# Weight sums of the seven-product blocks moved from GpSimd to VectorE, one norm over all tokens, and its values copied out of PSUM

## The chip, the cores and the metric

One core of a Trainium2 chip (trn2). The metric is the device time of one execution in microseconds (us), the median of several runs. The core's engines are named as in the profile: PE (TensorE, matmuls), DVE (VectorE), ACT (ScalarE), POOL (GpSimd) and SP (SyncE, which issues nearly all DMAs here). Each engine works through its own list of instructions in order, and waits on semaphores of the others.

## The reference, cut to what matters

One layer of a decoder for 576 tokens (512 of a prompt, 64 of samples), in float32: a half-step SwiGLU FFN, a token mixing with three branches, and another half-step FFN. The change touches the two FFNs and the norms at their two ends.

```python
D_MODEL = 1024; D_FF = 2816
def _rmsnorm(x, g):
    return x * lax.rsqrt(jnp.mean(x * x, axis=-1, keepdims=True) + RMS_EPS) * g
def _swiglu(x, w_up, w_down):
    hg = x @ w_up
    return (jax.nn.silu(hg[..., :D_FF]) * hg[..., D_FF:]) @ w_down
x = x + 0.5 * _swiglu(_rmsnorm(x, ffn1_norm), ffn1_w_up, ffn1_w_down)
m = _token_mixing(_rmsnorm(x, mix_norm), ...);  x = x + m
x = x + 0.5 * _swiglu(_rmsnorm(x, ffn2_norm), ffn2_w_up, ffn2_w_down)
y = _rmsnorm(x, final_norm)
```

## The kernel before, in words

Activations lie with channels on the 128 partitions and tokens on the free axis: a tile is 128 x 576, and is worked on in two halves of H = 288 tokens, since a PSUM bank takes 512 values. A float32 operand is split into two parts of the type fp32r (`split`, L95): ACT casts the high part (L96), and VectorE subtracts it from the value for the low part (L97). A product is then three matmuls: high by high, high by low, low by high (`mm3k`, L108, its matmuls at L110).

**An FFN** (`ffn`, L394) goes over 22 blocks of 128 hidden channels. Each block takes two tiles of up-weights (one for the silu side, one for the other), gives a hidden tile, and hidden tiles go into the down projection by groups of 6, 4, 4, 4 and 4 blocks (L447 adds the result to x). A group's down tiles are computed behind the next group's blocks, two for each block of a group of four.

- The first five blocks (`plain`, L434) multiply x·g that isn't yet normed, so that PE can start before the norm is known. The norm's factor rn of each token is applied when results leave PSUM: VectorE takes q·rn into t1 (L438), ACT applies silu (L439), GpSimd multiplies t1 by rn once more (L440), since the other side lacks that factor too, and VectorE multiplies the other side out of PSUM by t1 (L442).
- The other 17 blocks (`strassen`, L351) use seven half-size products over normed operands (`operands`, L320) in place of eight. Four sums of weight tiles are needed for a block, made by `total` (L357) on GpSimd: a21+a22 and a11+a21 read loaded weight tiles alone ("p<-w" in the profile; a11 and a12 lie in the block's first tile, a21 and a22 in its second), the two others read a sum and a weight tile ("p<-p,w"). `product` (L362) splits a sum or a weight tile into a pair (wh, wl) and runs 12 matmuls (L369). Results leave PSUM by ACT's copy m1 (L379) and VectorE's L380, L382, L384, L388 and L391; the first product of bank pb must be read (L380) before the t3 product may add to that bank. L471 multiplies the block's two sides.
- **The norm** (`norm`, L405): squares are summed over the channels' tiles on ACT and VectorE; PE sums them over partitions, 128 tokens at a time (L138, 128 x 1 each); VectorE, ACT and VectorE turn them into 1/sqrt (L299, L300 with a load of ACT's function table, L301); PE spreads the values over the partitions (L148), and ACT copies them to SBUF (L309). Before, this goes by halves: three pieces for each (128, 128 and 32 tokens), six in all.
- **The end of an FFN** (L481 on): the last group's down projections run half by half. The first half's norm is taken in between, and the next step's norm starts on it (`done`: `mix_norm`, L557, after the first FFN; `final`, L1106, after the second). There the factors stay in PSUM and are read from there (L563 in `mix_norm`).

Four pools of buffers matter: 4 buffers for loaded weight tiles (w), 4 for split pairs, 4 for sums (p), and 8 PSUM banks. The framework's scheduler sets each engine's order when the kernel is built, by its own cost model; so a move of work to another engine also moves its neighbours' order.

Of the kernel before, what the change touches and what calls it, by code (L numbers as in the profile page):

```python
# [6 lines left out]
F32 = mybir.dt.float32  # L7
F32R = mybir.dt.float32r
AF = mybir.ActivationFunctionType
ALU = mybir.AluOpType  # L10
# [8 lines left out]
N = SEQ + NB * TS  # L19
H = N // 2  # L20
# [30 lines left out]
class _Builder:  # L51
# [240 lines left out]
    def xg(self):  # L292
        return [[self.xp.tile([128, N], F32R, name=f"x{2 * k + i}") for i in range(2)] for k in range(8)]

    def rstd(self, fp, ss, h):

        q = self.sums("p", [ss], self.con("ones", 1), slice(h * H, (h + 1) * H))
        t = fp.tile([128, 3], F32, name="rt", bufs=2)
        self.V.tensor_scalar(t, q, 1.0 / D, 1e-6, ALU.mult, ALU.add)  # L299
        self.A.activation(t, t, AF.Sqrt)  # L300
        self.V.reciprocal(t, t)  # L301
        return t

    def rows(self, fp, t, h, r=None):

        (_, p), = self.spread("p", t.unsqueeze(2).broadcast_to([128, 3, 128]), slice(h * H, (h + 1) * H))
        if r is None:
            return p
        self.A.copy(r, p)  # L309
        return r  # L310

    def sumsq(self, fp, ss, x, k, s):
# [38 lines left out]
    def strassen(self, fp, w, xs):  # L351


        V, G, A = self.V, self.G, self.A
        a11, a12, a21, a22 = (t.rearrange("p (k e c) -> p k e c", e=2, c=128)[:, :, e, :] for t in w for e in range(2))

        def total(u, v):  # L357
            s = self.sp.tile([128, N], F32, name="p")[:, :512].rearrange("p (k c) -> p k c", c=128)
            G.tensor_tensor(s, u, v, ALU.add)  # L359
            return s  # L360

        def product(p, src, b, first):  # L362
            hl = self.wparts()
            v = [t.rearrange("p (k c) -> p k c", c=128) for t in hl]
            self.split(v[0], v[1], src)
            for k in range(4):
                c = slice(128 * k, 128 * k + 128)
                for q, (l, o) in enumerate(((0, 0), (0, 1), (1, 0))):
                    self.T.matmul(p, hl[l][:, c], xs[k][b][:, o], start=first and k == 0 and q == 0,  # L369
                                  stop=k == 3 and q == 2, skip_group_check=True)  # L370

        pa, pb, pc = (self.bank()[:, :H] for _ in range(3))
        m1 = fp.tile([128, H], F32, name="m1")
        t1, t2 = (fp.tile([128, N], F32, name=n) for n in ("t1", "t2"))
        p1 = total(a21, a22)
        p2 = total(p1, a11)
        product(pb, p2, "t2", True)
        product(pa, a11, "b11", True)
        A.copy(m1, pa)  # L379
        V.tensor_tensor(t1[:, H:], pb, m1, ALU.subtract)  # L380
        product(pc, p1, "t1", True)
        V.tensor_tensor(t2[:, H:], pc, m1, ALU.add)  # L382
        product(pb, total(a11, a21), "t3", False)
        V.tensor_tensor(t2[:, H:], pb, t2[:, H:], ALU.subtract)  # L384
        product(pa, a12, "b21", False)
        A.activation(t1[:, :H], pa, AF.Silu)
        product(pc, total(p2, a12), "b22", False)
        V.tensor_tensor(t1[:, H:], pc, t1[:, H:], ALU.subtract)  # L388
        A.activation(t1[:, H:], t1[:, H:], AF.Silu)
        product(pb, a22, "t4", False)  # L390
        V.tensor_tensor(t2[:, :H], pb, m1, ALU.subtract)  # L391
        return t1, t2

    def ffn(self, x, hp, fp, g, wu, wd, done, raw=None, mid=None, kv=()):  # L394
# [4 lines left out]
        V, A = self.V, self.A  # L399
        room = lambda s: [(self.xp if s < 8 else hp).tile([128, N], F32R, name=f"x{2 * s + i}") for i in range(2)]  # L400
        xg = self.xg()
        ss = self.sp.tile([128, N], F32, name="p")
        rn = fp.tile([128, N], F32, name="rn", bufs=1)

        def norm():  # L405
            for k in range(0 if not raw else 4, 8):
                self.sumsq(fp, ss, x[k], k, slice(0, N))
            r = [self.rstd(fp, ss, h) for h in range(2)]
            return [self.rows(fp, t, h, rn[:, h * H:(h + 1) * H]) for h, t in enumerate(r)]

        for k in range(8):
            gk = self.par(g, k)
# [2 lines left out]
            if raw:  # L415
# [7 lines left out]
                if k == 7:  # L423
                    r = norm()
# [3 lines left out]
        if not raw:  # L428
            pre = [self.proj(wu[i], xg) for i in range(2)]
            r = norm()  # L430
            pre.append(self.proj(wu[2], xg))
        up = lambda i: pre[i] if i < 3 else self.proj(wu[i], xg)

        def plain(f):  # L434

            t1, t2 = (fp.tile([128, N], F32, name=n) for n in ("t1", "t2"))
            for (c, q), ri in zip(up(2 * f), r):
                V.tensor_tensor(t1[:, c], q, ri, ALU.mult)  # L438
            A.activation(t1, t1, AF.Silu)  # L439
            self.G.tensor_tensor(t1, t1, rn, ALU.mult)  # L440
            for c, q in up(2 * f + 1):
                V.tensor_tensor(t2[:, c], q, t1[:, c], ALU.mult)  # L442
            return hidden(f, t2)

        def down(m, h, f0):
            for c, p in self.proj(wd[m, :, f0 * 128:(f0 + len(h)) * 128], h, len(h)):
                V.scalar_tensor_tensor(x[m][:, c], p, 0.5, x[m][:, c], ALU.mult, ALU.add)  # L447

        def hidden(f, t2):
            hj = room(ROOMS[f])  # L450
            self.split(hj[0], hj[1], t2)
            return hj

        first, xs = [], []
# [6 lines left out]
        for n in FGROUPS:  # L461
            h = []
            for j in range(n):
                f = f0 + j
                if f < PLAIN:
                    h.append(first[f])
                else:
                    w = nxt
                    nxt = self.raws(wu, f + 1) if f + 1 < NF else None
                    t1, t2 = self.strassen(fp, w, xs)  # L470
                    V.tensor_tensor(t2, t2, t1, ALU.mult)  # L471
                    h.append(hidden(f, t2))
                for m in behind[8 * j // n:8 * (j + 1) // n]:
                    m()
            behind = [(lambda m=m, h=h, f0=f0: down(m, h, f0)) for m in range(8)]
            f0 += n
        if mid:
            mid()
        w = []
        for m in range(8):  # L480
            o = self.xe.tile([128, 2, 2, H], F32R, name=("t1", "b11")[m // 4] + str(m % 4))  # L481
            w.append([o[:, i].rearrange("p i c -> p (i c)")[:, :n * 128] for i in range(2)])
            q = self.wtile()[:, :n * 128]
            self.dma(q, wd[m, :, (NF - n) * 128:])
            self.split(w[m][0], w[m][1], q)
        ss = self.sp.tile([128, N], F32, name="p")
        for i in range(2):
            s = slice(i * H, (i + 1) * H)
            for m in range(8):
                p = self.bank()[:, :H]  # L490
                self.mm3(p, lambda q, f, t: w[m][q][:, f:t], h, n, i)
                V.scalar_tensor_tensor(x[m][:, s], p, 0.5, x[m][:, s], ALU.mult, ALU.add)
                self.sumsq(fp, ss, x[m], m, s)
                if i == 1 and m == 2:
                    r = self.rstd(fp, ss, 0)
                if i == 1 and m == 4:
                    done(x, fp, slice(0, H), self.rows(fp, r, 0))
        if kv:
            kv[0]()
        r = self.rstd(fp, ss, 1)  # L500
        if kv:
            kv[1](0)
        r = self.rows(fp, r, 1)
        if kv:
            kv[1](1)
        done(x, fp, s, r)
# [725 lines left out]
```

## Time and profile before

| | |
|---|---|
| runs | 1503.19, 1508.43 and 1508.97 us, median 1508.43 |
| the profiled execution | 1504.17 us; its span from first to last instruction 1502.4 us |
| mean granted PE clock | 0.982 |
| PE busy | 97% of the span |
| VectorE busy | 67% |
| ACT busy | 45% |
| GpSimd busy | 14% |

The two FFNs take the first and the last part of the span (GpSimd, which works in them only, is busy up to slice 10 of 40 and again from slice 29), token mixing the middle. In a row of the profile, "x2" after a form is a run of equal instructions, the two numbers at its start are the time since the span's start and the duration in us, and brackets at its end give the idle time of the engine just before, and which engine's instruction ended it. A window's row gives the window, its width, the busy time of PE, PE's weight loads, VectorE, ACT and GpSimd, then the granted PE clock, the DMA engines' busy share and GB/s. A group's row gives the count, the busy time, the mean duration in ns, and the idle time before.

### The profile page before, as it was taken

What the parts mean: (1) busy time and instruction counts of PE and PEld (TensorE: products, weight loads), DVE (VectorE), ACT (ScalarE), POOL (GpSimd) and SP (SyncE); (2) the same over time, 40 slices, a digit from 0 to 9 for tenths busy, and PEclk for the clock granted to TensorE, in tenths of its full rate; (3) what the DMA queues carried; (4) which work ended last, traced back from release to release, by engine and by line L of the source; (5) the groups of instructions that cost most, each with busy time, mean ns of one, the idle gap of its engine ahead of it and who ended that gap; (6) DMA issues with size and microseconds to landing.
All of it is one profiled execution on the core that took longest, in us unless ns stands there. A gap on an engine that the chain in (4) does not pass through costs nothing.

```text
span 1502.4 us, 27187 instructions
## 1 busy us (share of the span) xinstructions
PE 1464.7 (97%) x10786; PEld 1380.1 (92%) x10786; DVE 1012.8 (67%) x1911; ACT 672.6 (45%) x1369; POOL 212.7 (14%) x167
## 2 busy tenths in 40 slices
PE   8989999999989999999999999999999999999997
PEld 8989999999988799888888878789999999999997
DVE  7976666666783569769456456356578766767665
ACT  6434333434566645445346542443344333444342
POOL 1233233222000000000000000000014222222310
PEclk9999999999999999999899999999999999999998
DMA  6223222223632154123223134255222322223231
GB/s 207 71 71 99 85 85 85 85 85 100 205 92 96 41 154 90 46 79 107 60 58 108 54 96 127 91 185 176 85 71 71 91 79 85 89 92 103 85 85 63
DMA packets 95034, 144.05 MB, mean 96 GB/s; under 512 B 43628, under 2 KB 53228, under 8 KB 94908
## 3 DMA queue, kind: packets, MB, share of 16 engines
q1 hardware_dynamic: 94332, 141.74, 30.6%
q8 instruction: 84, 1.38, 0.4%
q10 hardware_dynamic: 576, 0.59, 0.1%
q14 instruction: 42, 0.34, 0.1%
HBM read 126.07 MB, written 16.23 MB: 95 GB/s over the span
## 4 chain that ended last, share of the span: by engine, by line
PE 89%; DVE 5%; ACT 2%; issue 1%; DMA 1%; SPq 0%; DVEq 0%; ACTq 0%
PE p L110 51%; PE p L369 24%; DVE wl L97 2%; PE g L874 1%; PE c L1008 1%; ACT wh L96 1%; PE c L1012 1%; PE c L1005 1%; DVE pr L967 1%; PE g L128 1%; PE c L128 1%; PE c L1040 1%; PE p L148 1%; PE c L1038 1%; DMA w<-win 1%
## 5 line engine op out<-in xcount | busy, mean ns | idle before, releaser
L110 PE MATMUL p<-x,wh 128*128 128x288 f32 x3136 | 656.7, 301 | 5.1 <-ACT x L96 4.7
L110 PEld LDWEIGHTS p<-x,wh 128*128 128x128 f32 x3136 | 508.3, 189 | 19.0 <-issue 7.5
L110 PE MATMUL p<-x,wl 128*128 128x288 f32 x1568 | 470.3, 300 | 1.4 <-DVE wl L97 1.4
L97 DVE TENSOR_TENSOR wl<-w,wh 128x512 fp32r<-128x512 f32 (+1 forms) x353 | 270.9, 770 | 139.0 <-ACT wh L96 131.8
L96 ACT CAST wh<-w 128x512 fp32r<-128x512 f32 (+1 forms) x353 | 209.2, 599 | 245.1 <-PE p L369 109.4
L110 PEld LDWEIGHTS p<-x,wl 128*128 128x128 f32 x1568 | 296.0, 189 | 6.9 <-issue 3.1
L369 PE MATMUL p<-t,wh 128*128 128x288 f32 x1088 | 224.4, 299 | 7.6 <-DVE t L380 7.3
L369 PEld LDWEIGHTS p<-t,wh 128*128 128x128 f32 x1088 | 173.8, 188 | 15.5 <-DVE t L380 15.5
L369 PE MATMUL p<-b,wh 128*128 128x288 f32 x816 | 170.3, 295 | 0.6 <-ACT m L379 0.6
L369 PE MATMUL p<-t,wl 128*128 128x288 f32 x544 | 160.5, 295 | 0.0
L97 DVE TENSOR_TENSOR wl<-p,wh 128x512 fp32r<-128x512 f32 x136 | 109.6, 806 | 71.1 <-ACT wh L96 69.4
L359 POOL TENSOR_TENSOR p<-w 128x512 f32<-128x512 f32 x68 | 95.1, 1399 | 361.1 <-DVE wl L97 170.3
L96 ACT CAST wh<-p 128x512 fp32r<-128x512 f32 x136 | 84.2, 620 | 127.5 <-PE p L110 71.2
L369 PEld LDWEIGHTS p<-b,wh 128*128 128x128 f32 x816 | 132.8, 188 | 1.0 <-ACT m L379 0.9
L369 PE MATMUL p<-b,wl 128*128 128x288 f32 x408 | 120.4, 295 | 0.0
L440 POOL TENSOR_TENSOR t<-t,rn 128x576 f32<-128x576 f32 x10 | 17.8, 1789 | 715.8 <-ACT t L439 715.8
L359 POOL TENSOR_TENSOR p<-p,w 128x512 f32<-128x512 f32 x68 | 96.5, 1419 | 59.2 <-DVE wl L97 46.0
L369 PEld LDWEIGHTS p<-t,wl 128*128 128x128 f32 x544 | 102.4, 188 | 0.0
L369 PEld LDWEIGHTS p<-b,wl 128*128 128x128 f32 x408 | 76.8, 188 | 0.0
L96 ACT CAST x<-t 128x576 fp32r<-128x576 f32 (+1 forms) x60 | 36.4, 609 | 83.0 <-DVE t L471 69.1
L447 DVE SCALAR_TENSOR_TENSOR x<-p,x 128x288 f32<-128x288 f32 x128 | 56.6, 449 | 12.4 <-PE p L110 12.4
L97 DVE TENSOR_TENSOR x<-t,x 128x576 fp32r<-128x576 f32 (+1 forms) x60 | 44.3, 743 | 14.0 <-ACT x L96 13.6
(346 smaller groups left out, 2008.7 us busy)
## 6 DMA issues: line engine op xcount, KB each, us to landing
w<-wu SPq DMA_DIRECT2D x85, 512.0 KB
w<-win SPq DMA_DIRECT2D x44, 512.0 KB
w<-wd SPq DMA_DIRECT2D x64, 256.0 KB
w<-wd SPq DMA_DIRECT2D x16, 384.0 KB
d_mb<-gate SPq DMA_DIRECT2D x16, 288.0 KB
w<-wo SPq DMA_DIRECT2D x8, 512.0 KB
x<-x SPq DMA_DIRECT2D x8, 288.0 KB
d_x<-x SPq DMA_DIRECT2D x16, 144.0 KB
```

What stands on the lines that cost most here:

```text
L96: self.A.copy(hi, x)
L97: self.V.tensor_tensor(lo, x, hi.bitcast(F32), ALU.subtract)
L110: self.T.matmul(p, l, x[r][:, c], start=k == 0 and i == 0, stop=k == n - 1 and i == 2)
L128: self.T.matmul(p, l, r[:, c], start=i == 0, stop=i == len(ops) - 1)
L148: self.T.matmul(p[:, o + f - d.start:o + 128 - d.start], r[f:, i], self.con("ident")[f:, f:], start=True, stop=True)
L359: G.tensor_tensor(s, u, v, ALU.add)
L369: self.T.matmul(p, hl[l][:, c], xs[k][b][:, o], start=first and k == 0 and q == 0, stop=k == 3 and q == 2, skip_group_check=True)
L440: self.G.tensor_tensor(t1, t1, rn, ALU.mult)
L447: V.scalar_tensor_tensor(x[m][:, c], p, 0.5, x[m][:, c], ALU.mult, ALU.add)
L874: T.matmul(ps[:, i * 128:(i + 1) * 128], kb[o, c + i].rearrange("p a t -> p (a t)"), ra[o, c + i].rearrange("p a t -> p (a t)"), start=Tru ...
L967: V.tensor_tensor(pr, tt[:, :n, :e].unsqueeze(2).broadcast_to([np_, n, m, e]), l3[:, t:e, :e].unsqueeze(1).broadcast_to([np_, n, m, e]), A ...
L1005: T.matmul(ps[64:, 64 * h:64 * h + 64], gr[:64, h, c, 64:], vu[:64, c, 64 * h:64 * h + 64], start=h == 0 or not inter, stop=not inter)
```

## The change

Four things are changed.

1. `total` runs on VectorE: 136 sums of 128 x 512 (four for each of 34 blocks).
2. In `plain`, both sides leave PSUM times rn, and `hidden` multiplies them on VectorE (as L471 did for the other blocks). GpSimd's L440 is gone, and with it GpSimd's last work in the FFNs.
3. `norm` takes all 576 tokens at once: five pieces in place of six, one pass of VectorE, ACT and VectorE over them, and two copies (512 and 64 tokens).
4. At an FFN's end the first half's factors are copied by ACT to rn in SBUF, and in the first FFN the second half's too; there `mix_norm` reads SBUF. In the second FFN the last half's factors stay in PSUM as before.

```diff
-    def rstd(self, fp, ss, h):
-        q = self.sums("p", [ss], self.con("ones", 1), slice(h * H, (h + 1) * H))
-        t = fp.tile([128, 3], F32, name="rt", bufs=2)
+    def rstd(self, fp, ss, c):
+        q = self.sums("p", [ss], self.con("ones", 1), c)
+        t = fp.tile([128, 5], F32, name="rt", bufs=2)[:, :q.shape[1]]
...
-    def rows(self, fp, t, h, r=None):
-        (_, p), = self.spread("p", t.unsqueeze(2).broadcast_to([128, 3, 128]), slice(h * H, (h + 1) * H))
-        if r is None:
-            return p
-        self.A.copy(r, p)
+    def rows(self, t, c, r=None):
+        for d, p in self.spread("p", t.unsqueeze(2).broadcast_to([128, t.shape[1], 128]), c):
+            if r is None:
+                return p
+            self.A.copy(r[:, d.start - c.start:d.stop - c.start], p)
         return r
...
-            G.tensor_tensor(s, u, v, ALU.add)
+            V.tensor_tensor(s, u, v, ALU.add)
...
-            r = [self.rstd(fp, ss, h) for h in range(2)]
-            return [self.rows(fp, t, h, rn[:, h * H:(h + 1) * H]) for h, t in enumerate(r)]
+            c = slice(0, N)
+            self.rows(self.rstd(fp, ss, c), c, rn)
+            return [rn[:, h * H:(h + 1) * H] for h in range(2)]
...
-            for (c, q), ri in zip(up(2 * f), r):
-                V.tensor_tensor(t1[:, c], q, ri, ALU.mult)
-            A.activation(t1, t1, AF.Silu)
-            self.G.tensor_tensor(t1, t1, rn, ALU.mult)
-            for c, q in up(2 * f + 1):
-                V.tensor_tensor(t2[:, c], q, t1[:, c], ALU.mult)
-            return hidden(f, t2)
+            for i, t in enumerate((t1, t2)):
+                for (c, q), ri in zip(up(2 * f + i), r):
+                    V.tensor_tensor(t[:, c], q, ri, ALU.mult)
+                if i == 0:
+                    A.activation(t1, t1, AF.Silu)
+            return hidden(f, t1, t2)
...
-        def hidden(f, t2):
+        def hidden(f, t1, t2):
             hj = room(ROOMS[f])
+            V.tensor_tensor(t2, t2, t1, ALU.mult)
             self.split(hj[0], hj[1], t2)
...
-                    r = self.rstd(fp, ss, 0)
+                    r = self.rstd(fp, ss, slice(0, H))
                 if i == 1 and m == 4:
-                    done(x, fp, slice(0, H), self.rows(fp, r, 0))
+                    done(x, fp, slice(0, H), self.rows(r, slice(0, H), rn[:, :H]))
...
-        r = self.rows(fp, r, 1)
+        r = self.rows(r, s, rn[:, H:] if kv else None)
```

In the changed file L439 is the step out of PSUM times rn (for both sides), L450 the product in `hidden`, and L446 what L447 was; L359 and L380 to L391 keep their numbers.

The order on VectorE in the first FFN, from the last step of the plain blocks to the first seven-product block's L382, before. Names ending in a number are buffers: wl a low half of a pair, w a loaded weight tile, p a sum or a PSUM bank, x24 and x25 a hidden tile's two parts.

```order
L442 TENSOR_TENSOR t2_831<-p_906,t1_830 128x288
L97 TENSOR_TENSOR wl_1035<-p_996,wh_1034 128x512
L442 TENSOR_TENSOR t2_831<-p_931,t1_830 128x288
L97 TENSOR_TENSOR wl_1054<-p_1051,wh_1053 128x512
L97 TENSOR_TENSOR x25_959<-t2_831,x24_958 128x576
L97 TENSOR_TENSOR wl_1071<-w_982,wh_1070 128x512
L97 TENSOR_TENSOR wl_1090<-p_1087,wh_1089 128x512
L380 TENSOR_TENSOR t1_994<-p_991,m1_993 128x288
L382 TENSOR_TENSOR t2_995<-p_992,m1_993 128x288
```

The same place on VectorE after:

```order
L439 TENSOR_TENSOR t2_824<-p_923,rn_183 128x288
L97 TENSOR_TENSOR wl_1047<-p_1044,wh_1046 128x512
L450 TENSOR_TENSOR t2_824<-t2_824,t1_823 128x576
L359 TENSOR_TENSOR p_1187<-w_979,w_980 128x512
L97 TENSOR_TENSOR wl_1064<-w_975,wh_1063 128x512
L97 TENSOR_TENSOR x25_951<-t2_824,x24_950 128x576
L97 TENSOR_TENSOR wl_1083<-p_1080,wh_1082 128x512
L380 TENSOR_TENSOR t1_987<-p_984,m1_986 128x288
L359 TENSOR_TENSOR p_1223<-p_1134,w_979 128x512
L382 TENSOR_TENSOR t2_988<-p_985,m1_986 128x288
```

The step out of PSUM no longer stands behind GpSimd's product, but the product in `hidden` and a sum for the next block (reading w_979 and w_980) now stand ahead of L380, and another sum behind it.

A seven-product block in the middle of the first FFN on VectorE, from its L384 on, before:

```order
L384 TENSOR_TENSOR t2_2110<-p_2106,t2_2110 128x288
L97 TENSOR_TENSOR wl_2247<-w_2244,wh_2246 128x512
L97 TENSOR_TENSOR wl_2281<-w_2278,wh_2280 128x512
L388 TENSOR_TENSOR t1_2109<-p_2107,t1_2109 128x288
L97 TENSOR_TENSOR wl_2327<-p_2324,wh_2326 128x512
L391 TENSOR_TENSOR t2_2110<-p_2106,m1_2108 128x288
L97 TENSOR_TENSOR wl_2343<-w_2101,wh_2342 128x512
```

The same block on VectorE after:

```order
L384 TENSOR_TENSOR t2_2103<-p_2099,t2_2103 128x288
L97 TENSOR_TENSOR wl_2240<-w_2237,wh_2239 128x512
L97 TENSOR_TENSOR wl_2274<-w_2271,wh_2273 128x512
L359 TENSOR_TENSOR p_2315<-w_2095 128x512
L388 TENSOR_TENSOR t1_2102<-p_2100,t1_2102 128x288
L359 TENSOR_TENSOR p_2317<-p_2315,w_2094 128x512
L359 TENSOR_TENSOR p_2370<-w_2094,w_2095 128x512
L391 TENSOR_TENSOR t2_2103<-p_2099,m1_2101 128x288
L97 TENSOR_TENSOR wl_2320<-p_2317,wh_2319 128x512
```

Three sums for the next block now stand between this block's last steps out of PSUM. The first of them reads a weight tile that a DMA has just brought, and stands ahead of L388.

The norm of the second FFN on PE, between the second and third up-projection, before:

```order
L110 MATMUL p<-x_12129,wh 128x288
L110 MATMUL p<-x_12128,wl 128x288
L138 MATMUL p<-cst,p 128x1 x6
L148 MATMUL p<-cst,rt 128x128 x2
L148 MATMUL p<-cst,rt 128x32
L148 MATMUL p<-cst,rt 128x128 x2
L148 MATMUL p<-cst,rt 128x32
L110 MATMUL p<-x_12114,wh 128x288
```

The same place on PE after:

```order
L110 MATMUL p<-x_12124,wh 128x288
L110 MATMUL p<-x_12123,wl 128x288
L138 MATMUL p<-cst,p 128x1 x5
L148 MATMUL p<-cst,rt 128x128 x4
L148 MATMUL p<-cst,rt 128x64
L110 MATMUL p<-x_12109,wh 128x288
```

Six sums and six spreads have become five and five; their place is the same, and nothing else stands between the sums and the spreads.

More of the change, by code (lines that the diff above doesn't have):

```diff
@@ L351, in strassen @@
     def strassen(self, fp, w, xs):
-        V, G, A = self.V, self.G, self.A
+        V, A = self.V, self.A
         a11, a12, a21, a22 = (t.rearrange("p (k e c) -> p k e c", e=2, c=128)[:, :, e, :] for t in w for e in range(2))
@@ L469, in ffn @@
                     nxt = self.raws(wu, f + 1) if f + 1 < NF else None
-                    t1, t2 = self.strassen(fp, w, xs)
-                    V.tensor_tensor(t2, t2, t1, ALU.mult)
-                    h.append(hidden(f, t2))
+                    h.append(hidden(f, *self.strassen(fp, w, xs)))
                 for m in behind[8 * j // n:8 * (j + 1) // n]:
@@ L494, in ffn @@
                 if i == 1 and m == 2:
-                    r = self.rstd(fp, ss, 0)
+                    r = self.rstd(fp, ss, slice(0, H))
                 if i == 1 and m == 4:
-                    done(x, fp, slice(0, H), self.rows(fp, r, 0))
+                    done(x, fp, slice(0, H), self.rows(r, slice(0, H), rn[:, :H]))
         if kv:
             kv[0]()
-        r = self.rstd(fp, ss, 1)
+        r = self.rstd(fp, ss, s)
         if kv:
             kv[1](0)
-        r = self.rows(fp, r, 1)
+        r = self.rows(r, s, rn[:, H:] if kv else None)
         if kv:
```

## The prediction

> **What bounds the kernel now.** I read the page first, then the waits of PE for the whole run, then the same by stretch, then PE's, VectorE's and GpSimd's timelines where PE waits.
>
> ```profile
> PE 1464.7 (97%) x10786; PEld 1380.1 (92%) x10786; DVE 1012.8 (67%) x1911; ACT 672.6 (45%) x1369; POOL 212.7 (14%) x167
> 100.00:420.00 320.00, 319.80 (x2385) 316.19 (x2384) 219.09 (x384) 134.06 (x255) 79.18 (x56) 1.00 0.33 101
> 1110.00:1480.00 370.00, 366.46 (x2728) 362.46 (x2727) 265.01 (x424) 149.60 (x273) 98.76 (x71) 1.00 0.27 83
> ```
>
> PE is the bound. In 320 us of the first FFN (second row) it is busy for all but 0.2 us at clock 1.00; in 370 us of the second it misses 3.5 us. In such stretches a faster VectorE or an idle GpSimd is worth nothing. The change drops six norm matmuls and no others; the rest of a gain must be PE's idle time or clock.
>
> ```profile
> PE p L369 <- DVE t L380: 7.3, 8, 2.5
> PE p L369 <- ACT m L379: 0.6, 1, 0.6
> PE p L369 <- DVE t L380: 3.9, 2, 2.5
> PE p L369 <- DVE t L380: 3.4, 6, 1.4
> 80.42 0.40 PE L369 MATMUL p<-b,wh 128*128 128x288 f32 x1 [0.64 <-ACT m L379]
> 83.29 0.54 PE L369 MATMUL p<-t,wh 128*128 128x288 f32 x2 [2.48 <-DVE t L380]
> 96.25 0.53 PE L369 MATMUL p<-t,wh 128*128 128x288 f32 x2 [1.42 <-DVE t L380]
> ```
>
> The first two rows are PE's waits inside seven-product blocks over the whole run: total us, times, longest. The third is the part from 60 to 105 us, the fourth that from 1085 us on. So they lie in the first blocks of each FFN: 0.64 + 2.48 + 1.42 = 4.5 us in the first, 3.4 in the second, 7.9 together. PE waits for L380 to empty a PSUM bank. Why L380 is late, VectorE and GpSimd show:
>
> ```profile
> 76.90 0.46 DVE L442 TENSOR_TENSOR t<-p,t 128x288 f32<-128x288 f32 x1 [1.31 <-POOL t L440]
> 77.27 0.68 DVE L97 TENSOR_TENSOR wl<-p,wh 128x512 fp32r<-128x512 f32 x1
> 77.87 0.45 DVE L442 TENSOR_TENSOR t<-p,t 128x288 f32<-128x288 f32 x1
> 78.24 1.69 DVE L97 TENSOR_TENSOR wl<-p,wh 128x512 fp32r<-128x512 f32 x1
> 79.85 0.75 DVE L97 TENSOR_TENSOR x<-t,x 128x576 fp32r<-128x576 f32 x1
> 80.52 1.75 DVE L97 TENSOR_TENSOR wl<-w,wh 128x512 fp32r<-128x512 f32 x1
> 82.19 0.68 DVE L97 TENSOR_TENSOR wl<-p,wh 128x512 fp32r<-128x512 f32 x1
> 82.79 0.45 DVE L380 TENSOR_TENSOR t<-p,m 128x288 f32<-128x288 f32 x1
> 74.99 1.87 POOL L440 TENSOR_TENSOR t<-t,rn 128x576 f32<-128x576 f32 x1
> 78.09 1.29 POOL L359 TENSOR_TENSOR p<-p,w 128x512 f32<-128x512 f32 x1 [1.22 <-issue]
> 80.01 1.72 POOL L359 TENSOR_TENSOR p<-w 128x512 f32<-128x512 f32 x1 [0.63 <-DVE wl L97]
> ```
>
> The reader is to see two things. VectorE stood idle for 1.31 us until GpSimd's L440 was done. And the same subtraction of 128 x 512 takes 0.68 us alone but 1.69 and 1.75 us when a GpSimd sum lies beside it (78.09 to 79.38; 80.01 to 81.73): 1.01 + 1.07 = 2.08 us lost. L442, which reads PSUM, isn't stretched.
>
> **The change part by part.** VectorE's load first, since 136 sums move there.
>
> ```profile
> L97 DVE TENSOR_TENSOR wl<-w,wh 128x512 fp32r<-128x512 f32 x320 | 255.7, 801 | 127.1 <-ACT wh L96 120.3 <-ACT xs L1010 0.9 <-ACT rt L300 0.3
> L97 DVE TENSOR_TENSOR wl<-p,wh 128x512 fp32r<-128x512 f32 x136 | 109.6, 806 | 71.1 <-ACT wh L96 69.4
> 92.11 0.75 DVE L471 TENSOR_TENSOR t<-t,t 128x576 f32<-128x576 f32 x1
> ```
>
> A sum on VectorE is not in the trace; its nearest row is L97 of the same 128 x 512 with two SBUF operands, 0.68 alone, so 136 x 0.68 = 92.5 us, and 10 products of the plain blocks at 0.75 (L471 alone), 7.5. Back come the stretches: 320 x (0.801 - 0.68) + 136 x (0.806 - 0.68) = 55.9 us. VectorE goes from 1012.8 to 1012.8 + 92.5 + 7.5 - 55.9 = 1057 us, or some us less where the 576-wide steps are freed of stretch too, GpSimd to near nothing in the FFNs. No moved step issues a DMA, so no queue of SP or GpSimd changes its list. The densest stretch is 1110 to 1480: 17 blocks x 4 x 0.68 = 46 on 265 makes 311 of 370 even with no stretch given back. Where PE is full, all this is hidden under it.
>
> **The stalls.** In the first FFN's first block the new order puts, after the last step out of PSUM, a subtraction, L450, a sum, and three more subtractions (one of 128 x 576) ahead of L380: 0.68 + 0.75 + 0.68 + 0.68 + 0.74 + 0.68 = 4.2 us of durations, about 3.7 by the rows' start-to-start spacing (77.27 to 77.87 for a 0.68). Without L440's wait the last step out of PSUM can end some 1.3 us earlier than in L442's chain, near 75.4, so L380 starts at 79.1 to 79.6 and ends by 80.0, not 83.2. PE wanted that bank 2.48 us before 83.29, at 80.81, and m1's matmul 0.64 before 80.42, at 79.78: the latter needs a pair that ACT and VectorE can have ready at about 79.4. I keep 0.3 us a FFN, 0.6 of the 7.9: -7.3. Bounds: 0 (VectorE stays late all the same) and -7.9.
>
> In later blocks three sums stand between L384 and L391. What hides them: after the seventh product (12 matmuls at 319.80 / 2385 = 0.134, 1.6 us) stand two down tiles of the previous group, and PE's 100 to 420 row has no wait to start from. The first sum waits for a weight DMA at the head of VectorE's queue, with L388 behind it:
>
> ```profile
> 220.22 1.29 POOL L359 TENSOR_TENSOR p<-w 128x512 f32<-128x512 f32 x1 [11.83 <-DMA w<-wu]
> 220.65 0.46 DVE L388 TENSOR_TENSOR t<-p,t 128x288 f32<-128x288 f32 x1 [0.39 <-PE p L369]
> L359 POOL TENSOR_TENSOR p<-p,w 128x512 f32<-128x512 f32 x68 | 96.5, 1419 | 59.2 <-DVE wl L97 46.0 <-issue 5.9 <-DMA w<-wu 2.3
> L359 POOL TENSOR_TENSOR p<-w 128x512 f32<-128x512 f32 x68 | 95.1, 1399 | 361.1 <-DVE wl L97 170.3 <-DMA w<-wu 145.9 <-DVE x L447 18.7
> ```
>
> GpSimd waited 11.83 us for that tile; it came 0.43 us before L388 ran. So the sum would find its tile just there, and I cost this at 0 (bounds 0 and the slower rival below).
>
> **The norms.**
>
> ```profile
> 26.77 1.91 PE L148 MATMUL p<-cst,rt 128*128 128x128 f32 x12
> 1092.70 1.39 PE L138 MATMUL p<-cst,p 128*128 128x1 f32 x12
> 1093.40 1.28 ACT L300 ACT_TABLE_LOAD   x1
> 1095.17 3.27 PE L148 MATMUL p<-cst,rt 128*128 128x128 f32 x12 [1.07 <-DVE rt L301]
> 1092.00:1106.00 14.00, 12.93 (x75) 12.27 (x74) 8.80 (x18) 7.57 (x13) 1.95 (x1) 0.76 0.10 38
> ```
>
> A float32 matmul is two passes here, so six sums are 12 rows, 0.116 us each; five sums save 0.23 in the first FFN (same 1.39 there). The spreads go from 1.91 to an estimated 1.66: of six pieces two are of 32 tokens, of five one is of 64, so about 0.25. In the second FFN the spread runs at half clock, 3.27, and saves 0.45; its fewer sums save nothing, since after them PE waits 1.07 for a chain that begins with ACT's table load, begun during the sums. Together -0.9, bounds -0.3 and -1.3.
>
> In those 14 us the clock averaged 0.76: 14 x 0.24 = 3.4 us of full pace lost. So 1.39 of thin matmuls and 1.07 idle, 2.46 together, went before half clock, while the 2.48 us of idle in the first FFN left it whole:
>
> ```profile
> 78.00:90.00 12.00, 8.88 (x65) 8.43 (x64) 10.37 (x13) 5.35 (x11) 5.58 (x4) 1.00 0.27 89
> ```
>
> The chain's idle stays, so I keep that loss. By the Trainium skill (TensorE: Matmul & The Clock Gate, Part 1: The HAM clock gate (the "warmup" mystery)) the array falls to half clock after a whole idle window of about 3.4 us that runs freely. The first FFN's row agrees with that rule and the second's does not, as 2.46 us is less than such a window; by the rule alone the loss would be gone and the sum 3.4 us lower.
>
> **The ends of the FFNs.**
>
> ```profile
> 433.62 0.82 PE L110 MATMUL p<-x,wh 128*128 128x288 f32 x2 [4.71 <-ACT x L96]
> 27.74 0.40 ACT L309 COPY rn<-p 128x288 f32<-128x288 f32 x1 [1.29 <-PE p L148]
> L563 DVE SCALAR_TENSOR_TENSOR t<-x,pv,p 128x288 f32<-128x288 f32 x16 | 7.6, 507 | 0.5 <-PE p L148 0.3
> ```
>
> At the first FFN's end PE waits 4.71 us for the mixing norm's splits. A copy of 0.40 now stands on that path ahead of L563, plus its hand-over. What comes back: L563 reading SBUF, at best 8 x (0.507 - 0.45) = 0.44, only as far as ACT's casts aren't the gate. I take +0.4, bounds -0.4 and +1.0. In the second FFN the copied half lies under the second half's down projections: 0, bounds -0.3 and +0.3.
>
> **Sum:** -7.3 - 0.9 + 0.4 + 0 = -7.8 us. On the profiled execution: 1504.17 - 7.8 = 1496.4 (span 1494.6). That execution lies 4.26 below the median of the runs, 1508.43, on which the forecast stands: 1508.43 - 7.8 = 1500.6. About 0.5%, 7.5 us, is what a measurement of this kernel can tell from no change, so the forecast lies at that edge.
>
> **The rivals.**
>
> *Slower: a sum blocks VectorE's queue.* GpSimd's 145.9 us of waiting for w<-wu cost nothing, as nothing stood behind it; on VectorE L388, L391, the splits and the next L380 do. The DMA's landing now depends on when the weight buffer is freed, which VectorE's own subtraction and sum of the block before decide. PE's cover is what it still has queued: where no down tile stands behind the block, the seventh product and, if its pair is split by then, one more, 1.6 us each, so it decides from a landing 3.2 us after L388 could run. If PE lost 0.5 us in each of 32 later blocks: +16, 1516.6. For it: three sums stand together there. Against: the 0.43 us in hand, and DMA engines busy 0.33 and 0.27.
>
> *No gain: the stalls keep.* VectorE stays the late engine in the first blocks: 4 sums x 0.68 + 0.75 = 3.5 us come onto it per block where 1.31 of waiting and 2.08 of stretch go, 3.4. It is nearly even; only the order (sums behind L380) makes mine differ. Then 1508.43 - 0.9 + 0.4 = 1507.9. The Trainium skill (Perfetto Trace Analysis, Optimizing Scalar/DVE Operations) says that GpSimd and VectorE share a read port of SBUF, so that work moved between those two might not help; the 1.69 against 0.68 agrees that they share something, and this rival is what that rule would make here.
>
> *Faster: full clock in the second norm.* With one sum less the low stretch before the spread might stay short enough not to halve the clock, as 2.48 us of idle didn't: 3.4 more, 1508.43 - 7.8 - 3.4 = 1497.2. Against: only 0.23 us of 2.46 goes.
>
> **How the numbers follow.** Forecast 0.66, of which 0.36 beyond the 0.5% and 0.30 within, as 7.8 stands against 7.5; faster rival 0.12; no gain 0.12; slower 0.10. Faster 0.36 + 0.12 = 0.48, within 0.30 + 0.12 = 0.42, slower 0.10. Low end: the faster rival at the best bounds (stalls -7.9, norms -1.3, ends -0.7, clock -3.4: 1495.1), less the 4.26 by which a run lies below the median: about 1491. High end: no stalls gone, norms -0.3, ends +1.3: 1509.4. The slower rival lies outside.
>
> **What would show it.** Right: PE's waits on L380 and L379 in seven-product blocks under 1 us in all, subtractions of 128 x 512 at 0.68 in both groups, no GpSimd work in the FFNs, VectorE at 1045 to 1057 us, 0.76 again around the second norm, and about 5 us of wait at the first FFN's end. Wrong: L380 still named by PE, or a wait of a VectorE sum on w<-wu with PE idle behind it.

## The result, and the profile after

The changed kernel takes 1488.65 us in the median of 5 runs (1487.02 to 1489.83) against 1505.06 for the kernel before (1503.19 to 1508.97): a ratio of 0.9885, 95% interval 0.9864 to 0.9905. A second comparison (below) gave 0.9865, interval 0.9839 to 0.9890. By these ratios the gain is about 17 to 20 us where the prediction had 7.8; the time lies below the range given. The prediction stood on the median of the first three runs of before, 1508.43; five runs have their median at 1505.06.

The profiled execution took 1487.49 us, its span 1485.7, 16.7 less than before. First the page's first part and the two groups of weight subtractions, with the two groups of sums that are now on VectorE.

```profile
PE 1460.2 (98%) x10778; PEld 1378.1 (93%) x10778; DVE 1027.4 (69%) x2053; ACT 675.5 (45%) x1370; POOL 4.5 (0%) x21
L97 DVE TENSOR_TENSOR wl<-w,wh 128x512 fp32r<-128x512 f32 x320 | 218.4, 687 | 96.9 <-ACT wh L96 90.3 <-ACT xs L1008 0.9
L97 DVE TENSOR_TENSOR wl<-p,wh 128x512 fp32r<-128x512 f32 x136 | 93.5, 688 | 50.4 <-ACT wh L96 47.8
L359 DVE TENSOR_TENSOR p<-w 128x512 f32<-128x512 f32 x68 | 46.7, 686 | 3.2 <-DMA w<-wu 2.7
L359 DVE TENSOR_TENSOR p<-p,w 128x512 f32<-128x512 f32 x68 | 46.3, 681 | 0.1
```

The subtractions have fallen from 801 and 806 ns to 687 and 688, the value of one that runs alone. VectorE took on 93.0 us of sums and its busy time rose by only 14.6. The sums waited 2.7 us in all for weight DMAs, where GpSimd had waited 145.9.

Next PE's longest waits after, over the whole run (total us, times, longest). No row of a seven-product block (L369) is left, and of the 4.7 us ahead of the mixing stage 0.7 us are left, under another releaser.

```profile
PE p L110 <- ACT t L96: 5.5, 1, 5.5
PE p L148 <- DVE rt L301: 2.1, 2, 1.3
PE p L138 <- DVE p L318: 2.0, 1, 2.0
PE c L987 <- DMA aux<-s: 2.0, 1, 2.0
PE p L110 <- DVE wl L97: 1.5, 3, 1.1
...
PE p L110 <- ACT kv L541: 0.7, 1, 0.7
```

VectorE around the first seven-product block after, from the last step out of PSUM of the plain blocks to L382: the order that the prediction replayed, each instruction at its undisturbed duration.

```profile
74.46 0.45 DVE L439 TENSOR_TENSOR t<-p,rn 128x288 f32<-128x288 f32 x1
74.83 0.68 DVE L97 TENSOR_TENSOR wl<-p,wh 128x512 fp32r<-128x512 f32 x1
75.43 0.75 DVE L450 TENSOR_TENSOR t<-t,t 128x576 f32<-128x576 f32 x1
76.09 0.68 DVE L359 TENSOR_TENSOR p<-w 128x512 f32<-128x512 f32 x1
...
77.97 0.68 DVE L97 TENSOR_TENSOR wl<-p,wh 128x512 fp32r<-128x512 f32 x1
78.57 0.45 DVE L380 TENSOR_TENSOR t<-p,m 128x288 f32<-128x288 f32 x1
```

L380 starts at 78.57, 4.2 us earlier than before (0.5 of which the first norm's spread already had, 26.28 against 26.77), and PE doesn't wait for it.

**Where the 16.7 us came from.** The table takes each stage of PE between the norms' matmuls, from windows of 2 us: its width, PE's idle time in it, and the time lost to the clock (the sum of each window's width times one less its granted clock). The second and fourth columns are another execution of each kernel, from the experiments.

| stage: width / idle / lost to the clock, us | before | before, again | after | after, again |
|---|---|---|---|---|
| start to the first norm's spread | 26.8 / 5.9 / 0.0 | 27.1 / 5.7 / 0.0 | 26.3 / 5.5 / 0.0 | 27.1 / 5.9 / 0.0 |
| to the sums of the mixing norm's second half | 394.7 / 4.7 / 0.0 | 396.7 / 4.1 / 3.4 | 388.6 / 0.0 / 0.0 | 388.5 / 0.0 / 0.0 |
| first FFN's end and mixing, to the second FFN's norm | 671.2 / 13.3 / 20.5 | 670.3 / 14.4 / 18.8 | 667.6 / 9.5 / 20.5 | 664.8 / 9.7 / 17.1 |
| to the sums of the final norm's second half | 388.4 / 4.6 / 3.4 | 388.7 / 5.0 / 3.4 | 381.7 / 1.3 / 1.7 | 381.9 / 1.3 / 1.7 |
| to the end | 21.3 / 9.2 / 3.8 | 21.5 / 9.1 / 4.2 | 21.5 / 9.2 / 4.0 | 21.5 / 9.1 / 4.1 |
| sum | 1502.4 / 37.7 / 27.7 | 1504.3 / 38.3 / 29.8 | 1485.7 / 25.5 / 26.2 | 1483.8 / 26.0 / 22.9 |

Idle time repeats between executions to about 1 us; the clock's loss doesn't. Of the 16.7 us, 12.2 are idle time, 1.5 clock, and 3.0 is left for matmuls that are gone or run denser. By stage, 4.7 + 3.3 us of the idle time are the two FFNs, as forecast; 3.8 are in the stage that starts with the end of the first FFN, where a loss of 0.4 was forecast.

### The profile page after: what moved, and what is told of

Its sections match the earlier page's. It is cut to its first block, busy times and chain, and to the rows that moved or that the text cites. A ratio compares the mean times of both kernels' runs of the same rounds, so it can differ in the third digit from the quotient of the medians.

```text
span 1485.7 us, 27013 instructions
## 1 busy us (share of the span) xinstructions
PE 1460.2 (98%) x10778; PEld 1378.1 (93%) x10778; DVE 1027.4 (69%) x2053; ACT 675.5 (45%) x1370; POOL 4.5 (0%) x21
## 3 DMA queue, kind: packets, MB, share of 16 engines
q1 hardware_dynamic: 94332, 141.74, 30.9%
## 4 chain that ended last, share of the span: by engine, by line
PE 92%; DVE 4%; ACT 2%; DMA 1%; issue 1%; SPq 0%; DVEq 0%; ACTq 0%
PE p L110 51%; PE p L369 26%; PE g L872 1%; PE c L1006 1%; PE c L1010 1%; PE c L1003 1%; DVE pr L965 1%; PE g L128 1%; PE c L128 1%; PE c L1038 1%; PE c L1036 1%; DMA w<-win 1%; PE p L148 1%; PE c L1021 1%; PE c L1058 1%
## 5 line engine op out<-in xcount | busy, mean ns | idle before, releaser
L96 ACT CAST wh<-w 128x512 fp32r<-128x512 f32 (+1 forms) x353 | 209.5, 600 | 257.2 <-PE p L110 111.9
L97 DVE TENSOR_TENSOR wl<-w,wh 128x512 fp32r<-128x512 f32 (+1 forms) x353 | 231.9, 662 | 109.2 <-ACT wh L96 102.2
L369 PE MATMUL p<-t,wh 128*128 128x288 f32 x1088 | 224.2, 298 | 0.0
L369 PEld LDWEIGHTS p<-t,wh 128*128 128x128 f32 x1088 | 173.8, 188 | 6.4 <-DVE t L380 6.2
L369 PE MATMUL p<-b,wh 128*128 128x288 f32 x816 | 169.7, 295 | 0.0
L369 PE MATMUL p<-t,wl 128*128 128x288 f32 x544 | 160.5, 295 | 0.0
L96 ACT CAST wh<-p 128x512 fp32r<-128x512 f32 x136 | 84.5, 621 | 155.9 <-PE p L110 117.7
L369 PEld LDWEIGHTS p<-b,wh 128*128 128x128 f32 x816 | 132.6, 188 | 0.0
L97 DVE TENSOR_TENSOR wl<-p,wh 128x512 fp32r<-128x512 f32 x136 | 93.5, 688 | 50.4 <-ACT wh L96 47.8
L369 PE MATMUL p<-b,wl 128*128 128x288 f32 x408 | 120.3, 295 | 0.0
L369 PEld LDWEIGHTS p<-t,wl 128*128 128x128 f32 x544 | 102.4, 188 | 0.0
L369 PEld LDWEIGHTS p<-b,wl 128*128 128x128 f32 x408 | 76.8, 188 | 0.0
L446 DVE SCALAR_TENSOR_TENSOR x<-p,x 128x288 f32<-128x288 f32 x128 | 57.7, 451 | 20.3 <-PE p L110 20.3
L96 ACT CAST x<-t 128x576 fp32r<-128x576 f32 (+1 forms) x60 | 36.5, 610 | 45.6 <-DVE t L450 42.3
L1030 DVE SCALAR_TENSOR_TENSOR st<-c,gc,mg 64x64 f32<-64x64 f32 x56 | 15.9, 283 | 53.3 <-PE c L1021 52.5
L359 DVE TENSOR_TENSOR p<-w 128x512 f32<-128x512 f32 x68 | 46.7, 686 | 3.2 <-DMA w<-wu 2.7
L359 DVE TENSOR_TENSOR p<-p,w 128x512 f32<-128x512 f32 x68 | 46.3, 681 | 0.1
L110 PE MATMUL p<-x,t 128*128 128x288 f32 x264 | 38.5, 306 | 5.5 <-ACT t L96 5.5
```

The lines of the kernel that those rows point to most:

```text
L96: self.A.copy(hi, x)
L97: self.V.tensor_tensor(lo, x, hi.bitcast(F32), ALU.subtract)
L110: self.T.matmul(p, l, x[r][:, c], start=k == 0 and i == 0, stop=k == n - 1 and i == 2)
L359: V.tensor_tensor(s, u, v, ALU.add)
L1030: V.scalar_tensor_tensor(mn[s, s], ps[s, 256 + 64 * h:320 + 64 * h], gc[s, c:c + 1], mg[s, s], ALU.mult, ALU.add)
```

## The experiments

Ratios are to the kernel before, run beside each on the same chip, with 95% intervals. The theory formed from the two traces has two parts. First, GpSimd's sums stretched VectorE's subtractions, and so made L380 late. Second, the factors left in PSUM for the second half held up the mixing stage, whose PSUM pools take the place of the first FFN's; the copy frees them earlier. The rival to the second part is the prediction's own reading, that PE waits there for the mixing norm's splits. Below, the clock's loss of a run is its span multiplied by one less the mean granted clock, and span times clock is the span multiplied by the mean granted clock: what is left of the span without that loss.

### The copy of the second half's factors

Undone in the changed kernel:

```diff
-        r = self.rows(r, s, rn[:, H:] if kv else None)
+        r = self.rows(r, s, None)
```

> The changed kernel, but the second half's norm factors at the first FFN's end stay in PSUM as before the change (the copy on ACT is gone, the mixing norm reads PSUM). Theory (the copy frees the PSUM pool that the mixing stage's pools take over): PE's wait ahead of the first mixing matmul comes back, 0.7 to about 4.7 us, and with it the stretch at half clock behind it, some 1.5 us; 1488.7 + 5 = about 1494 us. Rival (PE waits for the mixing norm's splits, as the prediction had it, and the copy lies on that path): 0.4 us faster, 1488.3, the wait still about 0.7.

Measured: 1492.73 us, ratio 0.9919 (0.9896 to 0.9943). Its wait, from the waits of PE:

```profile
PE p L110 <- ACT x L96: 4.7, 1, 4.7
```

And PE in the 10 us around the wait's end, with the clock at 0.66:

```profile
426.00:436.00 10.00, 9.20 (x49) 9.23 (x50) 8.99 (x40) 2.69 (x8) 2.66 (x11) 0.66 0.37 96
```

The same place in the changed kernel has the whole clock:

```profile
422.00:432.00 10.00, 9.31 (x71) 9.12 (x70) 9.56 (x26) 7.46 (x20) 3.68 (x14) 1.00 0.51 122
```

The wait is back to the tenth of a microsecond, and 10 x 0.34 = 3.4 us of clock with it. The rival's gain of 0.4 didn't come. The clock goes with the wait in every profile: over the 10 us from the wait's end it is 0.70 to 0.85 in all seven executions that wait 4.7 us or more, and 1.00 in all seven that wait 0.7.

The copy alone, in the kernel before:

```diff
-        r = self.rows(fp, r, 1)
+        r = self.rows(fp, r, 1, rn[:, H:] if kv else None)
```

> The kernel before, with only the second half's factors copied out of PSUM at the first FFN's end. Theory (freed pool): the wait ahead of the first mixing matmul falls from 4.7 to about 0.7 us and the half-clock stretch goes, 1505.1 - 5 = about 1500 us; nothing else changes. Rival (splits): 1505.5.

Measured: 1495.4 us, ratio 0.9933 (0.9910 to 0.9956): about 10 us, twice what was expected. PE's waits: the stalls of the seven-product blocks are all there, and the wait ahead of mixing is 0.7.

```profile
PE p L369 <- DVE t L380: 7.1, 8, 2.5
...
PE p L110 <- ACT kv L543: 0.7, 1, 0.7
```

Idle time explains 4.0 of the 10. The rest lies in the clock: its loss averages 23.3 us over the 7 runs, and 31.0 over 46 runs of the kernel before in these comparisons (24.0 to 34.7).

A read that holds the PSUM without the norm's help: the norm reads SBUF, but a tiny product reads the factors' bank behind the last step.

```diff
             self.A.copy(r[:, d.start - c.start:d.stop - c.start], p)
+            self.last = p
...
         done(x, fp, s, r)
+        if kv:
+            V.tensor_tensor(fp.tile([128, 8], F32, name="late", bufs=1), self.t7[:, :8], self.last[:, :8], ALU.mult)
...
             self.split(self.xn[k][0][:, s], self.xn[k][1][:, s], t)
+            self.t7 = t
```

> The changed kernel with one tiny read by VectorE (128 x 8) of the second half's factors in PSUM put behind the mixing norm's last step; the norm itself still reads the copy in SBUF. Theory (freed pool): PE waits again ahead of the first mixing matmul until that read, about 5 to 6 us, and the half clock comes back, 1494 to 1496 us. Rival (what helped was that the norm reads SBUF, or the splits' order): no change, 1488.7.

Measured: 1492.47 us, ratio 0.9912 (0.9882 to 0.9942), a little below the expected 1494 to 1496. PE's longest wait, and PE in the 10 us behind it, where the clock is low again:

```profile
PE p L110 <- DVE late L507: 6.3, 1, 6.3
429.00:439.00 10.00, 9.78 (x58) 9.81 (x59) 9.72 (x48) 2.92 (x10) 2.61 (x11) 0.75 0.37 102
```

This separates the two theories: the splits and their source are the changed kernel's, only the bank is held longer, and PE waits 6.3 us for just that read, which ends 0.14 us ahead of the matmul.

### The sums, and the plain blocks

The sums alone, in the kernel before:

```diff
-            G.tensor_tensor(s, u, v, ALU.add)
+            V.tensor_tensor(s, u, v, ALU.add)
```

> The kernel before, with only the 136 weight sums moved from GpSimd to VectorE; GpSimd still multiplies by rn in the plain blocks. Theory (VectorE was late because GpSimd's sums stretched its subtractions): the second FFN's six waits on L380, 3.4 us, go, and of the first FFN's 4.5 at least 2.5; each stall that goes gives back about 0.2 us more than its idle, in restarting the matmuls; 5 to 8 us together, about 1499 us. Rival (VectorE stays late since 4 sums of 0.68 come onto it per block): waits on L380 of 4 us or more remain, 1503 to 1506. Rival (a sum blocks VectorE's queue): new waits in the later blocks, over 1506.

Measured: 1493.58 us, ratio 0.9926 (0.9904 to 0.9948), some 11 us where 5 to 8 were expected; the clock's loss is 27.6 us against 30.9 for the kernel before beside it. Of 7.9 us of stalls one is left:

```profile
PE p L369 <- DVE t L380: 0.9, 1, 0.9
```

That one is in the first FFN's first block, where VectorE still waits 1.3 us for GpSimd's product. No wait in the later blocks took its place.

The changed kernel with the sums back on GpSimd:

```diff
-            V.tensor_tensor(s, u, v, ALU.add)
+            self.G.tensor_tensor(s, u, v, ALU.add)
```

> The changed kernel with the 136 sums back on GpSimd. Theory (GpSimd's sums stretch VectorE's subtractions, which makes L380 late): subtractions of 128 x 512 back at about 0.80 mean, PE's waits on L380 and L379 back to 5 to 7.5 us, the wait of 0.7 us ahead of mixing stays; some 7 to 8.5 us slower than the changed kernel, 1496 to 1497. Rival (the plain blocks' new form was what ended the first FFN's stall): waits of 3.4 us in the second FFN only, 1492.

Measured: 1494.44 us, ratio 0.9922 (0.9902 to 0.9942), between the two expectations. Its waits and groups agree with the first theory:

```profile
PE p L369 <- DVE t L380: 6.2, 8, 1.4
```

```profile
L97 DVE TENSOR_TENSOR wl<-w,wh 128x512 fp32r<-128x512 f32 x320 | 253.1, 794 | 121.0 <-ACT wh L96 114.1 <-ACT xs L1008 0.9
```

The plain blocks' new form alone, in the kernel before (the second part of the change's diff, with the product in `plain`):

```diff
-            self.G.tensor_tensor(t1, t1, rn, ALU.mult)
...
+            V.tensor_tensor(t2, t2, t1, ALU.mult)
```

> The kernel before, with only the plain blocks' new form (both sides times rn out of PSUM, product on VectorE; GpSimd keeps the sums). Theory (stretch): the second FFN's 3.4 us of waits stay, the first FFN's 4.5 fall by the 1.3 that VectorE waited for GpSimd's product, less 0.75 that VectorE now does itself: 1 us or less, 1505. Rival (GpSimd's product was what made the first block late): the first FFN's 4.5 us go, 1500.

Measured: 1502.71 us, ratio 0.9971 (0.9956 to 0.9986), some 4 us where 1 or less was expected; 3.0 of it are the clock's loss (28.5 us against 31.5 beside it).

```profile
PE p L369 <- DVE t L380: 6.4, 9, 1.4
```

The longest stall falls from 2.5 to 1.4 us, and the first FFN's idle time from 4.7 to 3.0; the second FFN's waits stay. GpSimd's product was part of the first block's lateness, not the whole of it.

The stretch by itself: the changed kernel, where GpSimd makes each sum a second time into a buffer that is idle then (rn's; the expectation has VectorE's list as that of the changed kernel, but a few sums near the FFNs' first blocks stand elsewhere).

```diff
             V.tensor_tensor(s, u, v, ALU.add)
+            self.G.tensor_tensor(self.rn[:, :512].rearrange("p (k c) -> p k c", c=128), u, v, ALU.add)
             return s
...
-        rn = fp.tile([128, N], F32, name="rn", bufs=1)
+        self.rn = rn = fp.tile([128, N], F32, name="rn", bufs=1)
```

> The changed kernel, in which GpSimd makes each of the 136 sums a second time beside VectorE, into a buffer that nothing reads. VectorE's list is that of the changed kernel. Theory (stretch): VectorE's 128 x 512 subtractions and its sums get longer, 0.68 to 0.8 or more, waits on L380 come back, 5 us or more slower than the changed kernel, over 1493. Rival (only the order on VectorE and GpSimd's own delays counted): as the changed kernel, 1488.7.

Measured: 1545.86 us, ratio 1.0256 (1.0231 to 1.0282), far more than expected. PE's longest wait, then VectorE's groups:

```profile
PE p L370 <- DVE t L381: 44.6, 29, 5.3
```

```profile
L97 DVE TENSOR_TENSOR wl<-p,wh 128x512 fp32r<-128x512 f32 x136 | 122.9, 903 | 20.8 <-ACT wh L96 20.3
L359 DVE TENSOR_TENSOR p<-w 128x512 f32<-128x512 f32 x68 | 75.5, 1111 | 6.2 <-DMA w<-wu 5.5
L359 DVE TENSOR_TENSOR p<-p,w 128x512 f32<-128x512 f32 x68 | 70.3, 1034 | 0.0
```

Work that nothing reads, on an engine off the path, costs 57 us: VectorE's sums go from 686 and 681 to 1111 and 1034 ns, its subtractions of sums from 688 to 903 (those of loaded tiles only from 687 to 721), and L380 (L381 here) is late in 29 places. It costs more than the sums on GpSimd did before. The likely reason is that VectorE now carries the sums too and has less room for the stretch (1134.7 us busy, 1012.8 in the kernel before); no run tests that by itself.

### The norms

One norm over all tokens alone, in the kernel before (the third part of the change, written out in `norm`):

> The kernel before, with only the norm over all tokens at once at the start of each FFN. By the sums of the rows: 0.6 us in the first FFN and 0.5 to 0.7 in the second, 1505. If the half-clock stretch at the second norm hung on the sixth piece: 1.7 to 3.4 us more, 1502.

Measured: 1509.77 us, ratio 1.0016 (0.9998 to 1.0033): no gain that can be told, where 1 to 5 us were expected. The changed kernel with the norm by halves:

```diff
-            c = slice(0, N)
-            self.rows(self.rstd(fp, ss, c), c, rn)
-            return [rn[:, h * H:(h + 1) * H] for h in range(2)]
+            c = [slice(h * H, (h + 1) * H) for h in range(2)]
+            r = [self.rstd(fp, ss, i) for i in c]
+            return [self.rows(t, i, rn[:, i]) for t, i in zip(r, c)]
```

> The changed kernel, but the norm at the start of each FFN by halves as before (six pieces, two chains). By the rows: 0.6 us slower in the first FFN and 0.5 to 0.7 in the second, against 0.24 us less waiting for the chain: 1 us slower in all, which can't be told from none. If one norm costs something instead (alone it gave a ratio of 1.0016): up to 2.4 us faster.

Measured: 1485.31 us, ratio 0.9870 (0.9844 to 0.9897). Beside it ran the changed kernel itself:

> The changed kernel once more, on the chip of the next two. All theories: 0.988 to 0.990 of the kernel before. If the half-clock stretches are chance from execution to execution, its clock loss (span times one less the mean granted clock) scatters by several us about 26, and span times clock stays within 1.5 us.

Measured: 1484.87 us, ratio 0.9865 (0.9839 to 0.9890), a little below the expected 0.988. So one norm or two makes no difference that can be told, in either kernel. Its clock's loss averaged 24.0 us (20.7 to 28.3), and span times clock stayed in 1458.5 to 1461.5.

The first half's factors left in PSUM, in the changed kernel:

```diff
-                    done(x, fp, slice(0, H), self.rows(r, slice(0, H), rn[:, :H]))
+                    done(x, fp, slice(0, H), self.rows(r, slice(0, H)))
```

> The changed kernel, but the first half's norm factors at each FFN's end stay in PSUM as before. Theory (it is the last holder of the PSUM pool that counts, and the first half is done long before): no difference, within 0.2%. Rival (any factor left in PSUM holds the mixing stage up): the wait ahead of mixing grows from 0.7 to several us, 1492.

Measured: 1486.18 us, ratio 0.9866 (0.9845 to 0.9887): no difference, and the wait ahead of mixing stays 0.7. Only the last holder counts. None of these versions beats the changed kernel by more than its interval.

### The clock, in one kernel twice

> The kernel before once more, for a second profile of it. If the half-clock stretches are chance: PE's idle time per stage repeats to 0.5 us (4.7 in the first FFN, 13.3 in the end of the first FFN and mixing, 4.6 in the second FFN), while the clock loss per stage differs by whole stretches of 1.7 or 3.4 us.

Measured: 1506.13 us. Its stages are in the table above: idle time within 1.2 us of the first execution's in each (0.5 was expected), the clock's loss 3.4 us more in the first FFN and 1.7 less in mixing. PE from 78 to 90 us in it, across the same stall of the first block (2.47 us here, 2.48 in the first execution):

```profile
78.00:90.00 12.00, 8.86 (x45) 8.41 (x44) 8.39 (x11) 3.77 (x8) 5.56 (x4) 0.72 0.26 87
```

12 x 0.28 = 3.4 us are lost here; the prediction's row of the same window had 1.00.

## Why the prediction was wrong, point by point

**The end of the first FFN: the step that failed.** The prediction said that "PE waits 4.71 us for the mixing norm's splits" and that the copy stands on that path, +0.4; as a sign of being right it gave about 5 us of wait there, and 0.7 came. The row named ACT x L96, but a row names one releaser, the one nearest in time, and the trace of before spoke against it. The first mixing matmul reads the first half's splits, which VectorE had finished at 419.74 + 0.46 = 420.2. It started at 433.62, while splits of the second half were still to come. The last split of the first half, the last VectorE steps that read the factors in PSUM, and the first mixing matmul after:

```profile
419.74 0.46 DVE L97 TENSOR_TENSOR x<-t,x 128x288 fp32r<-128x288 f32 x1 [0.22 <-ACT x L96]
432.55 0.93 DVE L563 SCALAR_TENSOR_TENSOR t<-x,pv,p 128x288 f32<-128x288 f32 x2
422.96 0.53 PE L110 MATMUL p<-x,wh 128*128 128x288 f32 x2 [0.69 <-ACT kv L541]
```

The L563 steps end at 433.48, 0.14 us ahead of the matmul of before. The instruction lists say it as well: the first mixing matmul, before and after (DVE_49 and Activation_49 are semaphores of VectorE and ACT).

```
L110 MATMUL p_5322<-x0_4928,wh_5314 128x288 [waits DVE_49,Activation_49]
L110 MATMUL p_5317<-x0_4922,wh_5309 128x288 [waits Activation_49]
```

Followed to the instructions that raise them, the wait on DVE_49 is for the last L563, which reads the factors' bank, and that on Activation_49 before is for ACT's last copy of kv out of PSUM (L543, done at 429.3): no split is among them. After, the wait for VectorE is gone. The mixing stage opens PSUM pools of its own (3, 2 and 3 banks) in the place of the first FFN's 8; until the second half's factors were read for the last time, its first matmul could not start. Measured: 4.71 to 0.69 us of idle time, and 1.7 to 3.4 us of clock behind it (0.76 over 7 us in the first execution of before, 0.66 over 10 us in the kernel with the copy undone, 1.00 after). So at that place the term was -4.0 of idle and with the clock -5.7 to -7.4, not +0.4. The stage as a whole shows less of the clock's part: its loss to the clock was 20.5 us both before and after in the first pair of executions, 18.8 and 17.1 in the second, and it became 3.6 and 5.5 us shorter. The late read shows the mechanism; the prediction's bound of -0.4 on this term came from L563's duration, which didn't change (507 to 511 ns).

**The clock: put at no change.** The prediction kept the clock's loss as it was, on the ground that the idle time in the second norm's chain stays. Over the runs that loss fell from 31.0 to 26.5 and 24.0 us, 4.5 to 7.0 less. With the 4.4 us between +0.4 and -4.0 and some 1.6 more for the stalls (next paragraph) that is about what the gain has beyond the forecast. The place behind the wait and that of the first block's stall account for part of it; the rest is open (below).

**The stalls: right, and somewhat small.** The prediction had -7.3 of 7.9 us of idle time; all 7.9 went. The replay of the first block put L380 at 79.1 to 79.6, the trace has 78.57, in an execution that came to the first spread 0.5 us earlier. Two things were left out. A stall costs more than its idle time: between the first FFN's spread and the spread of the next norm's first half, 2802 matmuls took 376.63 us of PE before, and 2803 took 375.61 after, 1.0 us for three stalls (so 0.3 for each, not the 0.2 of the expectation above). And the stall of 2.5 us halves the clock for 3.4 us of loss in some executions (before again, the copy alone and the one norm alone show 0.72 in that window) and not in others, as in the one that the prediction read. Stalls of 1.4 us (the plain form alone, the sums back on GpSimd) left it at 1.00.

**The norms: right in the rows, nothing in the time.** The prediction counts six dropped matmuls; the lists have four, a sum and a spread in each FFN, eight rows of PE (10786 to 10778). Its sum doesn't hang on that. The first FFN's sums fell from 1.39 to 1.17 us and its spread from 1.91 to 1.50, the second's wait grew from 1.07 to 1.31. PE at the second FFN's norm after:

```profile
1082.46 1.17 PE L138 MATMUL p<-cst,p 128*128 128x1 f32 x10
1084.95 2.50 PE L148 MATMUL p<-cst,rt 128*128 128x128 f32 x10 [1.31 <-DVE rt L301]
1082.00:1096.00 14.00, 12.69 (x86) 12.26 (x85) 8.48 (x19) 9.15 (x15) 0.00 (x0) 0.88 0.11 39
```

The clock averages 0.88 over these 14 us, 14 x 0.12 = 1.7 lost instead of 3.4. But the runs don't tie that to the norm: kernels with one norm lost 0.0 to 3.4 us there (0.0 with the copy undone, 3.4 with the late read and with one norm alone), those with two 1.7 to 3.4. So the whole clock of the faster rival does occur, and nothing shows that the sixth piece decides it.

**VectorE's load: over-estimated.** 1045 to 1057 us were forecast, 1027.4 came. Besides the two groups reckoned with, other steps between two SBUF operands were freed too (L471, now L450, from 845 to 750 ns). And neighbours in VectorE's list overlap: in the rows above a step of 0.68 us is followed by the next after 0.60. Added up by the groups' durations the rise is 29.0 us, as busy time of the engine 14.6.

**The rivals.** A sum that blocks VectorE's queue: refuted here. The sums waited 2.7 us in all for weight tiles, and PE has no wait in a seven-product block. No gain, because VectorE is already full: refuted by the changed kernel, which has no stall left, and by the sums alone (7.9 us of stalls to 0.9). The prediction set beside it a rule from the Trainium skill (Perfetto Trace Analysis, Optimizing Scalar/DVE Operations), that work moved between VectorE and GpSimd might not help. The runs agree that the two hinder each other (1111 against 686 ns); but here moving all of the work to VectorE helped.

**What stays open.** Over its runs the kernel before lost 31.0 us to the clock on average, the changed one 26.5 and 24.0 in its two comparisons, the copy alone 23.3. What happens at the first FFN's end gives up to 3.4 of that, the first block's stall up to 3.4 in some executions. Most of the rest is lost inside the mixing stage, whose instructions the change doesn't touch. The kernel with the late read, with 6.3 us of idle time, averaged 25.4 over four runs, so a longer wait at that place doesn't by itself mean more loss; why the copy alone gained 10 us rather than 6 isn't settled. The parts don't add up either: the sums, the copy and the plain form gave ratios of 0.9926, 0.9933 and 0.9971 alone, product 0.9831, against 0.9885 and 0.9865 together; the intervals allow some of that difference. The excess lies in the clock: in span times clock, each against the kernel before beside it, the three parts take off 8.3, 2.7 and 1.1 us, together 12, and the changed kernel in its second comparison 14.1.

## What to carry to other kernels

Where a stage's first instruction waits, ask of each operand and of each buffer it writes who holds it last; the releaser that a row names may be only the one nearest in time. A value left in PSUM to save a copy holds its pool until its last reader, and where the next stage's pools take that place the copy is cheap. Before moving work between VectorE and GpSimd, compare the same instruction with and without the other engine beside it, and ask where the difference falls. Here a GpSimd sum that met a subtraction had cost VectorE 1 us, more than the 0.68 of the sum on VectorE. Over all 136 sums it was less: the two groups of subtractions gave back 53.4 us, 0.4 for each sum, against 93.0 taken on. The move paid because the stretch had fallen where L380 was already late, and the added work fell where PE was covered.

## What the runs showed of the hardware that wasn't expected

A VectorE instruction between two SBUF operands of 128 x 512 takes 0.68 us alone, and averaged 1.03 to 1.11 us with a GpSimd sum of the same size beside it; steps of 128 x 288 that read PSUM stayed at 0.45. TensorE's clock fell after 2.5 us of idle time in the same kernel in one execution (0.72 over 12 us) and not in another (1.00). In the stages of the table up to the final norm the losses differ by steps of 1.7 and 3.4 us. Two executions of one kernel differ by up to 10 us (1500.46 to 1510.26 over 23 runs), while span times mean clock scatters by half as much (1471.0 to 1475.2). The Trainium skill (TensorE: Matmul & The Clock Gate, Part 1: The HAM clock gate (the "warmup" mystery)) has windows of about 3.4 us that run freely, which agrees with both the steps (half of 3.4 is 1.7) and the chance; that a whole window must be idle doesn't agree with 2.5 us.
